# Input norm of a decoder trunk: squares on two engines, the first weights' load behind a copy, one exponential behind the last root

## The chip, the cores and the metric

The kernel runs on one core of one Trainium2 chip. A core has five engines with an instruction queue each: TensorE (PE, matrix products and transposes), VectorE (DVE), ScalarE (ACT), GpSimd (POOL) and SyncE (SP, which only issues DMAs here). Each engine takes its own instructions strictly in order, and semaphores make them wait for one another. The metric is the device time of one launch in microseconds. Three runs of the kernel before took 1421.04, 1417.68 and 1419.02 us.

## The reference

All data are float32, with SEQ = 512 rows of D_MODEL = 1024. A gated DeltaNet layer comes first, then an MLP with a short convolution, a K/V projection that is made once, an attention layer with a sliding window, a second MLP and a last norm. The change touches the very start, the norm of the input and what hangs on it:

```python
def rmsnorm(x, w):
    xf = x.astype(jnp.float32)
    y = xf * lax.rsqrt(jnp.mean(xf * xf, axis=-1, keepdims=True) + EPS)
    return (y * w.astype(jnp.float32)).astype(x.dtype)

def gated_deltanet(hn, w_in, conv_w, a_log, dt_bias, out_norm_w, w_out):
    proj = hn @ w_in
    qkv, z, b, a = jnp.split(proj, ...)
    qkv = jax.nn.silu(causal_dwconv(qkv, conv_w))
    q, k, v = jnp.split(qkv, [GDN_QK_DIM, 2 * GDN_QK_DIM], axis=-1)
    ...
    beta = jax.nn.sigmoid(b)
    g = -jnp.exp(a_log) * jax.nn.softplus(a + dt_bias)
    o = chunked_gated_delta_rule(q, k, v, g, beta)
    o = rmsnorm(o, out_norm_w) * jax.nn.silu(z)
    return o.reshape(bsz, t, GDN_V_DIM) @ w_out
```

## The kernel before

**Products.** Each float32 operand is split into a high part (rounded to the format that TensorE takes at full rate) and a low part (the rest). A product is three matmuls, high by high, low by high and high by low: L162, L163 and L164 in `mm3`, whose names `xh`, `xl` are the split input and `whi`, `wlo` the split weights. A projection of 128 columns sums over KD = 8 blocks of rows, so it is 24 matmuls into one PSUM bank `d` (128x512). Weights come in pieces of 256 columns into `stage` (two buffers, 1 MB each), and `cast` makes `whi` on ScalarE (L132) and `wlo` on VectorE (L133), 128 columns at a time, in three buffers each.

**The opening.** SP loads x in four pieces `xt` of 128 rows (L204, 512 KB each), then the first weights in two halves (L210). For each piece a square with a row sum (L258) and a root (L259) run on ScalarE, a reciprocal (L260) and the scaling (L261) on VectorE. TensorE transposes the scaled pieces (L266) into eight banks of four blocks each. `split_scaled` writes `xh` on ScalarE (L172) and `xl` on VectorE (L173). `columns` (L226 to 238) loads small vectors, transposes them (L235) and copies them out (L237): `normc` is the norm's weight, `cwc` the convolution's, and `onwc` and `fcw` others.

**After it.** The first projections are `d` of keys (128 columns each), then the gates (48 columns, weights `gst`, loaded by ScalarE's own queue in two transfers with runs of 64 bytes, L309 and L310). `conv_silu` takes a first tap on ScalarE (L277), three taps on VectorE (L280) and Silu on ScalarE (L281). The gate chain runs Sigmoid (L325), Abs (L326), Relu (L330), Exp (L327) and Ln (L328) on ScalarE, then an addition (L331), a product with `nega` (L332; `nega` is the exponential of a_log, L319), running sums (L335) and differences (L338) on VectorE, and copies to `gr` (L344 to L347). Functions of different tables on ScalarE need a table load between them, shown as ACT_TABLE_LOAD.

**The delta rule** works on four groups of heads: a triangular inverse built by levels (L576 to L615: products of 32x32 and 64x64 blocks on TensorE, with copies `pz` and `p6s` on ScalarE and writes into `sy` on VectorE between them), and a scan over four blocks of rows (L635 to L679). Projections for the next group stand between its steps on TensorE. Behind the last group the output projection multiplies `kT` and `qT` (high and low part of the gated output, which comes back from memory) by the next weights.

**What sets the order.** The kernel is written against a tile framework whose scheduler orders the instructions of each engine from a table of steps (ORDER, SHIFT), from its own estimate of when each could start, and from `behind(later, earlier)`, which fixes an order of issue and adds no wait. An edit at the start can therefore move instructions much later.

## Time and profile before

| what | value |
|---|---|
| runs of the kernel before | 1417.68, 1419.02, 1421.04 us (median 1419.02) |
| the profiled execution: its time, its span | 1418.66 us, 1416.8 us |
| granted TensorE clock, mean | 0.998 |
| TensorE busy | 1384.8 us, 98% |
| VectorE busy | 1109.1 us, 78% |
| ScalarE busy | 748.0 us, 53% |
| GpSimd busy | 15.7 us, 1% |

The span runs from the first to the last instruction; the profiled execution's time is 1.9 us longer than its span. "Busy" is the time in which an engine executes something. A group's row names the line, the engine, the operation and the tiles (output, arrow, inputs). In the timeline each row has start, duration and, in brackets, how long the engine was idle before and what ended the idle time.

### The profile page before, as it was taken

To read this page: it belongs to the slowest core of one execution; us is meant where nothing else is said; L and a number is where in the kernel's file an instruction comes from. 1 tells how busy PE (TensorE), PEld (TensorE's weight loads), DVE (VectorE), ACT (ScalarE), POOL (GpSimd) and SP (SyncE) were. 2 spreads that over 40 slices of the span, in tenths; PEclk is the share of its full clock that TensorE was granted. 3 is DMA by queue.
4 is the path that set the end of the run, shared out by engine and by line. 5 is a ranking of instruction groups with operands and counts; after the bars stand their busy time and mean duration, and the time that the engine had idled before them with its cause. 6 is when DMAs were issued, how large, how long until landed. Compare 5 with 4: busy or idle time off the path is not lost.

```text
span 1416.8 us, 21740 instructions
## 1 busy us (share of the span) xinstructions
PE 1384.8 (98%) x8362; PEld 1166.5 (82%) x8362; DVE 1109.1 (78%) x2072; ACT 748.0 (53%) x1470; POOL 15.7 (1%) x37
## 2 busy tenths in 40 slices
PE   7999999999999999999999999999999999999997
PEld 5787888878877888888988889778788888988897
DVE  4996886968856447879878889788658888878996
ACT  7764576656647325444335446567544444444543
POOL 1000000000100000000000000000000000000000
PEclk9999999999999999999999999999999999999999
DMA  5333254172465323221443223322132221432222
GB/s 160 90 104 115 80 174 124 60 230 84 143 221 157 119 86 115 90 90 46 134 149 119 75 73 108 109 76 76 60 112 86 93 90 59 137 107 86 95 75 75
DMA packets 162299, 151.80 MB, mean 107 GB/s; under 512 B 24148, under 2 KB 150677, under 8 KB 162197
## 3 DMA queue, kind: packets, MB, share of 16 engines
q1 hardware_dynamic: 159938, 150.22, 33.0%
q8 instruction: 66, 1.08, 0.3%
q10 hardware_dynamic: 2259, 0.20, 0.1%
q14 instruction: 36, 0.29, 0.1%
HBM read 133.60 MB, written 15.75 MB: 105 GB/s over the span
## 4 chain that ended last, share of the span: by engine, by line
PE 85%; DVE 7%; DMA 4%; ACT 2%; issue 1%; SPq 0%; DVEq 0%; ACTq 0%
PE d L162 20%; PE d L164 20%; PE d L163 20%; PE g L198 2%; DVE wlo L133 2%; PE d L1207 1%; PE d L1211 1%; PE d L1209 1%; PE d L1054 1%; PE d L1052 1%; PE d L1053 1%; PE s L1054 1%; PE p L1303 1%; PE s L659 1%; PE s L1052 1%
## 5 line engine op out<-in xcount | busy, mean ns | idle before, releaser
L162 PE MATMUL d<-xh,whi 128*128 128x512 f32 x1128 | 444.2, 394 | 0.2
L163 PE MATMUL d<-xl,whi 128*128 128x512 f32 x1128 | 444.0, 394 | 0.0
L164 PE MATMUL d<-xh,wlo 128*128 128x512 f32 x1128 | 442.1, 393 | 0.8 <-DVE wlo L133 0.5
L132 ACT CAST whi<-stage 128x1024 fp32r<-128x1024 f32 (+2 forms) x234 | 227.4, 976 | 249.7 <-PE d L163 170.3
L133 DVE TENSOR_TENSOR wlo<-stage,whi 128x1024 fp32r<-128x1024 f32 (+2 forms) x234 | 263.3, 1128 | 70.2 <-ACT whi L132 69.3
L164 PEld LDWEIGHTS d<-xh,wlo 128*128 128x128 f32 x1128 | 211.6, 188 | 45.5 <-DVE wlo L133 1.0
L162 PEld LDWEIGHTS d<-xh,whi 128*128 128x128 f32 x1128 | 211.7, 188 | 44.8 <-ACT xh L172 0.5
L163 PEld LDWEIGHTS d<-xl,whi 128*128 128x128 f32 x1128 | 211.7, 188 | 43.1 <-issue 0.5
L280 DVE SCALAR_TENSOR_TENSOR acc<-d,cwc,acc 128x511 f32<-128x511 f32 (+2 forms) x96 | 70.6, 738 | 8.7 <-ACT acc L277 7.8
L913 DVE TENSOR_TENSOR sz<-d,p6s 128x512 f32<-128x512 f32 x59 | 40.6, 688 | 43.4 <-PE d L164 41.2
L935 ACT ACTIVATE dt<-dt 128x512 f32<-128x512 f32 x44 | 27.8, 632 | 78.3 <-DVE dt L918 78.3
L918 DVE SCALAR_TENSOR_TENSOR dt<-sz,fcw,dt 128x511 f32<-128x511 f32 (+1 forms) x60 | 44.8, 747 | 1.8 <-ACT dt L916 0.9
L918 DVE SCALAR_TENSOR_TENSOR va<-sz,fcw,va 128x511 f32<-128x511 f32 (+1 forms) x58 | 43.3, 747 | 0.9
L561 DVE TENSOR_TENSOR sT<-sT,p6s 64x31 f32<-64x31 f32 (+15 forms) x124 | 40.9, 330 | 2.0
L555 DVE TENSOR_TENSOR p6s<-sN,sT 64x31 f32<-64x31 f32 (+15 forms) x124 | 40.7, 328 | 1.9
L1276 ACT ACTIVATE dt<-dt,sm 128x256 f32<-128x256 f32 (+1 forms) x64 | 30.1, 471 | 21.5 <-DVE sm L1259 21.5
L132 ACT CAST whi<-st 128x768 fp32r<-128x768 f32 (+1 forms) x30 | 23.7, 791 | 30.1 <-PE p L1053 5.8
L913 DVE TENSOR_TENSOR zl<-d,p6s 128x512 f32<-128x512 f32 x29 | 20.0, 688 | 17.8 <-PE d L164 17.8
L682 ACT ACTIVATE rq<-o 128x128 f32<-128x128 f32 x64 | 19.0, 301 | 25.0 <-DVE o L677 22.0
L937 DVE TENSOR_TENSOR va<-dt,va 128x512 f32<-128x512 f32 x44 | 30.4, 690 | 1.2
L133 DVE TENSOR_TENSOR wlo<-st,whi 128x768 fp32r<-128x768 f32 (+1 forms) x30 | 26.8, 899 | 2.2 <-ACT whi L132 2.2
L916 ACT ACTIVATE dt<-sz,normc,fcw 128x512 f32<-128x512 f32 x30 | 24.4, 815 | 6.5 <-DVE sz L913 6.2
(769 smaller groups left out, 2873.2 us busy)
## 6 DMA issues: line engine op xcount, KB each, us to landing
stage<-in_ffn_w_up_dram SPq DMA_DIRECT2D x44, 1024.0 KB, 4.7
stage<-in_a_w_in_dram SPq DMA_DIRECT2D x23, 1024.0 KB, 5.5
stage<-in_ffn_w_down_dram SPq DMA_DIRECT2D x16, 768.0 KB, 4.3
stage<-in_a_w_out_dram SPq DMA_DIRECT2D x8, 1024.0 KB, 5.1
st<-in_ffn_w_down_dram SPq DMA_DIRECT2D x8, 768.0 KB, 5.2
zd<-sz SPq DMA_DIRECT2D x16, 256.0 KB, 2.6
od<-o SPq DMA_DIRECT2D x16, 256.0 KB
stage<-in_b_w_q_dram SPq DMA_DIRECT2D x4, 1024.0 KB, 5.0
```

The lines of the kernel that those rows point to most:

```text
L132: S.copy(hi[:, :kt, :m], src)
L133: V.tensor_tensor(lo[:, :kt, :m], src, hi[:, :kt, :m].bitcast(F32), op=ALU.subtract)
L162: PE.matmul(ps, hi[:, k, :m], xh[k], start=first and k == 0, stop=False)
L163: PE.matmul(ps, hi[:, k, :m], xl[k][:], start=False, stop=False)
L164: done.append(PE.matmul(ps, lo[:, k, :m], xh[k], start=False, stop=last and k == kt - 1))
L280: V.scalar_tensor_tensor(acc[:, d:], ps[:, : T - d], col, acc[:, d:], op0=ALU.mult, op1=ALU.add)
L555: V.tensor_tensor(tv, N[:, s, s + 1 : 32].unsqueeze(2).to_broadcast([64, n, m]), Tm[:, s : s + 1, 0:m].to_broadcast([64, n, m]), op=ALU.mult,)
L561: V.tensor_tensor(Tm[:, s + 1 : 32, 0:m], Tm[:, s + 1 : 32, 0:m], tv, op=ALU.subtract)
L913: V.tensor_tensor(u[:], ps[:], rs[:], op=ALU.mult)
L918: V.scalar_tensor_tensor(acc[:, d:], u[:, : T - d], tap(2 - d, t), acc[:, d:], op0=ALU.mult, op1=ALU.add)
L937: V.tensor_tensor(b[:], a[:], b[:], op=ALU.mult)
L1276: S.activation(ej, ej, AF.Exp, bias=ngm[:, i : i + 1], scale=-1.0, accum_out=den[:, i : i + 1])
```

## The change

It does three things. The first weights' load is issued behind a copy on ScalarE, which reads two columns of the third x piece and writes two elements of the stage buffer, so that the load must wait for that copy (and the copy for the piece). The squares of the second and fourth piece (c = 1 and 3) run on VectorE as a product with a running sum, with the sum read out by a second instruction; the others stay on ScalarE. The exponential for `nega` is put behind the last root in the order of issue.

```diff
--- before.py
+++ after.py
@@ -205,14 +205,16 @@
         xs.append(xt)
     win = a_w_in[0]
     first = wpool.tile([P, 8, 256], F32, tag="stage", bufs=2, name=nm("stage"))
+    held_stage = {HQK * P: first}
+
+
+    ident = const([P, P], s="ident")
+    make_identity(nc, ident[:])
+
+    S.copy(first[:, 0, 0 : P + 1 : P], xs[2][:, 0:2])
     for i in range(2):
         cs = slice(HQK * P + i * P, HQK * P + (i + 1) * P)
         SP.dma_start(first[:, :, i * P : (i + 1) * P], win[:, cs].rearrange("(k p) c -> p k c", p=P))
-    held_stage = {HQK * P: first}
-
-
-    ident = const([P, P], s="ident")
-    make_identity(nc, ident[:])
     identr = const([P, P], F32R, s="identr")
     S.copy(identr[:], ident[:])
     ones = const([P, P], s="ones")
@@ -255,8 +257,21 @@
     for c in range(NC):
         junk = main.tile([P, D], F32, tag="nt", bufs=2, name=nm("junk"))
         r = const([P, 1], s="rx")
-        S.activation(junk[:], xs[c], AF.Square, accum_out=r[:])
-        S.activation(r[:], r[:], AF.Sqrt, bias=epsc[:, 0:1], scale=1.0 / D)
+
+        if c % 2 == 0:
+            S.activation(junk[:], xs[c], AF.Square, accum_out=r[:])
+        else:
+            V.tensor_tensor_reduce(
+                out=junk[:],
+                in0=xs[c][:],
+                in1=xs[c][:],
+                scale=1.0,
+                scalar=0.0,
+                op0=ALU.mult,
+                op1=ALU.add,
+                accum_out=r[:],
+            )
+        root = S.activation(r[:], r[:], AF.Sqrt, bias=epsc[:, 0:1], scale=1.0 / D)
         V.reciprocal(r[:], r[:])
         V.tensor_scalar(xs[c][:], xs[c][:], r[:, 0:1], None, op0=ALU.mult)
     xh, xl = [], []
@@ -316,7 +331,7 @@
     SP.dma_start(gp16[32:48, 0:1], a_a_log.rearrange("a h -> h a"))
     SP.dma_start(gp16[32:48, 1:2], a_dt_bias.rearrange("a h -> h a"))
     nega = const([48, 1], s="nega")
-    S.activation(nega[32:48, :], gp16[32:48, 0:1], AF.Exp)
+    behind(S.activation(nega[32:48, :], gp16[32:48, 0:1], AF.Exp), root)
     V.tensor_scalar(nega[32:48, :], nega[32:48, :], -1.0, None, op0=ALU.mult)
     R = row("sz")
     G.memset(R[0:80, :], 0.0)
```

Lines move by 2 near the start and by 15 behind the norm: the square is L262 (ScalarE) or L264 (VectorE, printed as ISA, with `rx` its sum), the root L274, the reciprocal L275, the scaling L276, the transposes L281, the taps L292 and L295, the addition L346, the differences L353, the levels L600 to L630, the scan's products L666 and L674. All names get a number one higher.

**The opening on VectorE**, from behind the two constants up to the first `xl`. xt_70, xt_72, xt_74 and xt_76 are the four pieces. Before:

```order
L260 RECIPROCAL rx_105<-rx_105 128x1
L261 TENSOR_SCALAR xt_70<-xt_70,rx_105 128x1024
L260 RECIPROCAL rx_111<-rx_111 128x1
L261 TENSOR_SCALAR xt_72<-xt_72,rx_111 128x1024
L260 RECIPROCAL rx_117<-rx_117 128x1
L261 TENSOR_SCALAR xt_74<-xt_74,rx_117 128x1024
L237 COPY normc_102<-g_100 128x128
L260 RECIPROCAL rx_123<-rx_123 128x1
L261 TENSOR_SCALAR xt_76<-xt_76,rx_123 128x1024
L133 TENSOR_TENSOR wlo_209<-stage_78,whi_208 128x1024
L173 SCALAR_TENSOR_TENSOR xl_134<-s_128,normc_102,xh_133 128x512
```

With the change, up to the first weights' low part:

```order
L264 ISA junk_111,rx_112<-xt_72 128x1024
L264 ISA rx_112 128x1
L275 RECIPROCAL rx_106<-rx_106 128x1
L276 TENSOR_SCALAR xt_70<-xt_70,rx_106 128x1024
L275 RECIPROCAL rx_112<-rx_112 128x1
L276 TENSOR_SCALAR xt_72<-xt_72,rx_112 128x1024
L275 RECIPROCAL rx_118<-rx_118 128x1
L264 ISA junk_123,rx_124<-xt_76 128x1024
L264 ISA rx_124 128x1
L239 COPY normc_103<-g_101 128x128
L276 TENSOR_SCALAR xt_74<-xt_74,rx_118 128x1024
L275 RECIPROCAL rx_124<-rx_124 128x1
```

The square of the second piece stands ahead of everything; that of the fourth stands between the reciprocal and the scaling of the third.

**The opening on ScalarE**, from the third piece to the first `xh`. whi_208 or whi_209 is the first projection's weight, whi_247 or whi_248 the gates'. Before:

```order
L258 ACTIVATE junk_116,rx_117<-xt_74 128x1024
L259 ACTIVATE rx_117<-rx_117,eps_90 128x1
L217 CAST identr_86<-ident_81 128x128
L258 ACTIVATE junk_122,rx_123<-xt_76 128x1024
L309 DMA gst_243<-in_a_w_in_dram 128x8x16
L259 ACTIVATE rx_123<-rx_123,eps_90 128x1
L132 CAST whi_208<-stage_78 128x1024
L310 DMA gst_243<-in_a_w_in_dram 128x8x16
L172 ACTIVATE xh_133<-s_128,normc_102 128x512
```

With the change:

```order
L214 COPY stage_78<-xt_74 128x2
L262 ACTIVATE junk_117,rx_118<-xt_74 128x1024
L274 ACTIVATE rx_118<-rx_118,eps_91 128x1
L219 CAST identr_87<-ident_79 128x128
L324 DMA gst_244<-in_a_w_in_dram 128x8x16
L325 DMA gst_244<-in_a_w_in_dram 128x8x16
L274 ACTIVATE rx_124<-rx_124,eps_91 128x1
L132 CAST whi_209<-stage_78 128x1024
L132 CAST whi_248<-gst_244 128x8x48
L172 ACTIVATE xh_134<-s_129,normc_103 128x512
```

The cast of the gates' weights has moved from behind the fifth `xh` to a place ahead of the first, and the second gate transfer from behind a weight cast to right behind the first transfer.

**The gate chain on VectorE**, from the third projection's weights to the fourth's; acc_236 and acc_413 are conv rows, va and sz the gate chain, wlo_545 and wlo_636 the low weights of the third and fourth projection of keys and queries. Before:

```order
L280 SCALAR_TENSOR_TENSOR acc_236<-d_207,cwc_204,acc_236 128x511
L280 SCALAR_TENSOR_TENSOR acc_236<-d_207,cwc_204,acc_236 128x510
L280 SCALAR_TENSOR_TENSOR acc_236<-d_207,cwc_204,acc_236 128x509
L133 TENSOR_TENSOR wlo_545<-stage_541,whi_544 128x1024
L133 TENSOR_TENSOR wlo_636<-stage_632,whi_635 128x1024
L331 TENSOR_TENSOR va_284<-va_284,va_289 16x512
L280 SCALAR_TENSOR_TENSOR acc_413<-d_384,cwc_204,acc_413 128x511
L332 TENSOR_SCALAR va_289<-va_284,nega_279 16x512
L280 SCALAR_TENSOR_TENSOR acc_413<-d_384,cwc_204,acc_413 128x510
L335 SCALAR_TENSOR_TENSOR sz_282<-ones_88,va_289 16x128 x4
L338 TENSOR_SCALAR sz_282<-sz_282 16x128 x4
```

With the change, from the second tap of the first conv row:

```order
L295 SCALAR_TENSOR_TENSOR acc_237<-d_208,cwc_205,acc_237 128x510
L133 TENSOR_TENSOR wlo_546<-stage_542,whi_545 128x1024
L295 SCALAR_TENSOR_TENSOR acc_237<-d_208,cwc_205,acc_237 128x509
L295 SCALAR_TENSOR_TENSOR acc_414<-d_385,cwc_205,acc_414 128x511
L346 TENSOR_TENSOR va_285<-va_285,va_290 16x512
L295 SCALAR_TENSOR_TENSOR acc_414<-d_385,cwc_205,acc_414 128x510
L347 TENSOR_SCALAR va_290<-va_285,nega_280 16x512
L295 SCALAR_TENSOR_TENSOR acc_414<-d_385,cwc_205,acc_414 128x509
L350 SCALAR_TENSOR_TENSOR sz_283<-ones_89,va_290 16x128 x4
L353 TENSOR_SCALAR sz_283<-sz_283 16x128 x4
L133 TENSOR_TENSOR wlo_637<-stage_633,whi_636 128x1024
L133 TENSOR_TENSOR wlo_672<-stage_633,whi_671 128x1024
```

wlo_636 stood ahead of the chain; as wlo_637 it stands behind all of it.

**The same place on TensorE**, at the start of the fourth projection, with d_634 or d_635 its bank. Before:

```order
L162 MATMUL d_634<-xh_133,whi_635 128x512
L163 MATMUL d_634<-xl_134,whi_635 128x512
L164 MATMUL d_634<-xh_133,wlo_636 128x512
L162 MATMUL d_634<-xh_142,whi_635 128x512
L163 MATMUL d_634<-xl_143,whi_635 128x512
L164 MATMUL d_634<-xh_142,wlo_636 128x512
```

With the change:

```order
L162 MATMUL d_635<-xh_134,whi_636 128x512
L163 MATMUL d_635<-xl_135,whi_636 128x512
L162 MATMUL d_670<-xh_134,whi_671 128x512
L163 MATMUL d_670<-xl_135,whi_671 128x512
L164 MATMUL d_635<-xh_134,wlo_637 128x512
L162 MATMUL d_635<-xh_143,whi_636 128x512
L163 MATMUL d_635<-xl_144,whi_636 128x512
```

Two products of the projection behind it have been put ahead of the first that needs wlo_637.

**The last group of the delta rule on TensorE**, near 407 to 411 us of the profile before, with p_4050 and s_4061 the last level's banks, s_4133 the scan's first product. Before:

```order
L605 MATMUL p_4050<-Xg,nt_3418 64x64 x8
L162 MATMUL d_4404<-xh_169,whi_4405 128x512
L163 MATMUL d_4404<-xl_170,whi_4405 128x512
L164 MATMUL d_4404<-xh_169,wlo_4406 128x512
L612 MATMUL s_4061<-sy_4001,p6s_347 64x64 x8
L651 MATMUL s_4133<-vt_3773,sy_3929 128x128 x2
L162 MATMUL d_4404<-xh_178,whi_4405 128x512
L651 MATMUL s_4133<-vt_3866,sy_4001 128x128 x2
L163 MATMUL d_4404<-xl_179,whi_4405 128x512
L164 MATMUL d_4404<-xh_178,wlo_4406 128x512
L162 MATMUL d_4404<-xh_187,whi_4405 128x512
L163 MATMUL d_4404<-xl_188,whi_4405 128x512
```

With the change, from the same product on:

```order
L620 MATMUL p_4051<-Xg,nt_3419 64x64 x8
L627 MATMUL s_4062<-sy_4002,p6s_348 64x64
L666 MATMUL s_4134<-vt_3774,sy_3930 128x128 x2
L627 MATMUL s_4062<-sy_4002,p6s_348 64x64 x7
L162 MATMUL d_4626<-kT_4479,whi_4627 128x512
L162 MATMUL d_4684<-kT_4479,whi_4685 128x512
L163 MATMUL d_4626<-qT_4480,whi_4627 128x512
L164 MATMUL d_4626<-kT_4479,wlo_4628 128x512
L163 MATMUL d_4684<-qT_4480,whi_4685 128x512
L162 MATMUL d_4626<-kT_4479,whi_4627 128x512
L666 MATMUL s_4134<-vt_3867,sy_4002 128x128 x2
```

The products of the last gate projection that stood between the levels now run earlier, and six of the output projection (d_4626, d_4684) stand there.

## Prediction

> **What bounds the kernel now.** I read four views in this order: the page's busy shares and chain of waits, the table of what TensorE waited for, the busy time in windows of 40 us, and the timeline of the opening, of 30 to 46 us and of 410 to 426 us.
>
> ```profile
> span 1416.8 us, 21740 instructions
> PE 1384.8 (98%) x8362; PEld 1166.5 (82%) x8362; DVE 1109.1 (78%) x2072; ACT 748.0 (53%) x1470; POOL 15.7 (1%) x37
> ...
> PE 85%; DVE 7%; DMA 4%; ACT 2%; issue 1%; SPq 0%; DVEq 0%; ACTq 0%
> ```
> ```profile
> engine line waited for: us in total, times, longest us
> PE g L235 <- DMA xt<-in_x_dram: 8.5, 1, 8.5
> ...
> PE d L162 <- ACT kT L168: 2.0, 1, 2.0
> PE g L235 <- DVE onwc L237: 1.7, 1, 1.7
> PE g L198 <- ACT ol L720: 1.5, 1, 1.5
> PE p L659 <- ACT us L653: 1.5, 1, 1.5
> ```
> ```profile
> 0.00:40.00 40.00, 30.56 (x134) 23.04 (x135) 21.01 (x36) 29.72 (x45) 6.01 (x17) 1.00 0.45 142
> 40.00:80.00 40.00, 38.25 (x197) 31.02 (x196) 37.07 (x75) 30.95 (x68) 0.00 (x0) 1.00 0.39 114
> ...
> 280.00:320.00 40.00, 38.48 (x266) 30.43 (x266) 29.03 (x56) 22.96 (x47) 0.00 (x0) 1.00 0.66 204
> ...
> 400.00:440.00 40.00, 36.56 (x326) 30.19 (x325) 23.43 (x52) 24.11 (x75) 0.61 (x2) 1.00 0.65 212
> ```
>
> TensorE (PE) is busy 1384.8 of 1416.8 us, and its work is the same afterwards, so the new time is the old one plus the change in its idle time. The idle is 9.4 us before 40 us, 1.75 at 40 to 80, 1.5 at 280 to 320 and 3.4 at 400 to 440 (window less its first busy figure). The waits name each: 8.5 until the input, 1.7 for the copy of onwc, 1.5 for the scaled ol, 2.0 and 1.5 inside the last group of the delta rule. The change reorders instructions up to about 440 us; behind that the order is unchanged, so an idle microsecond won or lost before then reaches the end whole.
>
> **The opening, as it runs.** The timeline's columns are start, duration, engine, line, operation, and in brackets the wait:
>
> ```profile
> 8.16 1.06 ACT L258 ACTIVATE junk<-xt 128x1024 f32<-128x1024 f32 x1 [0.94 <-DMA xt<-in_x_dram]
> ...
> 9.34 0.29 ACT L259 ACTIVATE rx<-rx,eps 128x1 f32<-128x1 f32 x1
> ...
> 9.73 1.05 ACT L258 ACTIVATE junk<-xt 128x1024 f32<-128x1024 f32 x1
> ...
> 9.87 0.75 DVE L261 TENSOR_SCALAR xt<-xt,rx 128x1024 f32<-128x1024 f32 x1
> ...
> 10.92 0.40 ACTq L310 DMA_DIRECT2D gst<-in_a_w_in_dram  x1
> ...
> 11.11 1.03 ACT L132 CAST whi<-stage 128x1024 fp32r<-128x1024 f32 x1
> ...
> 11.44 0.75 DVE L261 TENSOR_SCALAR xt<-xt,rx 128x1024 f32<-128x1024 f32 x1
> ...
> 12.17 1.23 DVE L133 TENSOR_TENSOR wlo<-stage,whi 128x1024 fp32r<-128x1024 f32 x1
> ...
> 12.89 0.69 ACT L172 ACTIVATE xh<-s,normc 128x512 fp32r<-128x512 f32 x1 [0.75 <-PE s L266]
> ...
> 13.62 0.75 DVE L173 SCALAR_TENSOR_TENSOR xl<-s,normc,xh 128x512 fp32r<-128x512 f32 x1 [0.22 <-ACT xh L172]
> 13.63 0.80 PE L162 MATMUL d<-xh,whi 128*128 128x512 f32 x1
> ...
> 16.16 0.50 ACT L132 CAST whi<-gst 128x384 fp32r<-128x384 f32 x1
> ...
> 18.29 0.39 PE L162 MATMUL d<-xh,whi 128*128 128x512 f32 x1
> ```
> ```profile
> 0.00:8.00 8.00, 0.00 (x0) 0.00 (x0) 1.07 (x5) 4.15 (x8) 4.14 (x13) 1.00 0.75 273
> ```
>
> **Weights held back: worth nothing to x.** In the first 8 us the core moved 273 GB/s x 8 us = 2.18 MB. The four pieces of x are 2.10 MB and the constants of ScalarE's queue 0.07, so the weights, issued behind x on the same queue, had not begun. The last square starts at 9.73 without waiting for x4: ScalarE was only then free. So x lands as before. [...] The copy (128x2, estimated 0.2 us from the page's small ScalarE rows such as the 0.29 root) starts when the third piece is there, 8.16; SP then issues the weights at about 8.4 rather than 4.27, and they land an estimated 0.3 to 1 us later, about 11.5. The weight cast started at 11.11 and now stands behind a root at 11.7, which covers it.
>
> **Squares on VectorE: a loss of about 1.1 us to the first product.** No row shows the reduce at this size. Its bounds are 0.75 (a VectorE pass of 128x1024 with one input, L261) and 1.92 (four times the 480 ns that a custom VectorE reduction takes for 128x256); I take 1.23, from the two-input pass of the same size (L133), plus 0.1 for reading the accumulator:
>
> ```profile
> L1259 DVE CUSTOM_DVE_ANT_0 dt<-s,sz,nsink x40: 344/479/484, 934.5 to 1004.6; 128x256 f32<-128x256 f32 x30, 128x128 f32<-128x128 f32 x10
> ```
>
> The square of x2 is hidden (5.7 to 7.0, while x3 still moves). That of x4 is not, since VectorE's order puts it behind the reciprocal of piece 3 and ahead of piece 3's scaling. The square of x3 on ScalarE ends 0.2 later for the copy, so its root ends at 9.8 and the reciprocal at 10.0; the square of x4 runs 10.05 to 11.4; normc's copy follows; scaling of x3 starts at 11.7 (before: 9.87); root, reciprocal and scaling of x4 end at 13.3 (before: 12.19). Four transposes later xh starts at about 14.0 against 12.89. On ScalarE the cast of the gate weights (0.50, formerly 16.16) now stands ahead of that xh, at about 13.5: their second transfer is issued some 0.5 earlier than 10.92, so I cost it at nothing, covered by the wait for x4.
>
> From the first product to 18.29 TensorE has little slack, but part of it ran slow: 0.80 for the product at 13.63 against 0.39 at 18.29. If the fast clock comes at the same absolute time, about 16, some 0.65 is won back. One gates product goes ahead into a wait (0.23, the spacing of products). So the dense stretch starts 1.1 - 0.65 = 0.45 later and the gates end 0.25 later. Bounds: +0.1 and +1.4 (nothing won back, 0.3 more for the gate cast). The exponential behind the last root costs nothing either way: before, it stood at 18.29, behind all roots already; it now stands two xh earlier, and all xh are still ready ahead of their products.
>
> **The gate chain: TensorE's new wait.** The next weights leave 1.5 earlier (their SP issue waited for the gates' wlo, which moves ahead of two xl), without use: the cast had other waits. The rows of the second place:
>
> ```profile
> 26.47 1.28 ACT L281 ACT_TABLE_LOAD   x1
> ...
> 31.60 1.28 ACT L327 ACT_TABLE_LOAD   x1
> ...
> 34.61 1.28 ACT L328 ACT_TABLE_LOAD   x1
> 34.63 1.23 DVE L133 TENSOR_TENSOR wlo<-stage,whi 128x1024 fp32r<-128x1024 f32 x1 [6.92 <-ACT whi L132]
> ...
> 36.66 0.68 DVE L331 TENSOR_TENSOR va<-va,va 16x512 f32<-16x512 f32 x1 [0.81 <-ACT va L328]
> ...
> 39.57 0.39 PE L164 MATMUL d<-xh,wlo 128*128 128x512 f32 x1
> ...
> 40.89 0.87 DVE L338 TENSOR_SCALAR sz<-sz 16x128 f32<-16x128 f32 x4
> ...
> 45.96 0.48 PE L235 MATMUL g<-ident,f 128*128 128x128 f32 x2 [1.72 <-DVE onwc L237]
> ```
>
> Before, wlo of the fourth projection ran at 34.63, five us ahead of its product at 39.57. Now it stands behind the whole gate chain on VectorE. That chain starts 0.45 later, loses about 1.2 because wlo of the third projection (1.23) slips between its first taps, so that the Silu table (26.47), which waits for the last tap, loads at 27.3 or later; between Exp and Ln a conv row (0.69) replaces a weight cast (1.05), -0.4. The addition then starts at 37.0 (36.66), a tap each stands between the steps as before, and the four L338 rows end near 42.0 (41.76). wlo runs 42.0 to 43.2. TensorE reaches the product at 39.57 + 0.25 + two pulled-ahead products (0.46) = 40.3 and waits **2.9 us**. In return the 1.72 at 45.96 goes: the rows between (13 products, 2.96, the transposes 0.6, two products 0.46) bring TensorE to fcw at 47.3, and onwc, behind two wlo, gr, a tap and a third wlo (1.2 + 0.7 + 0.7 + 1.2 = 3.9 behind 43.2), is there at 47.2. So 47.3 against 45.96: **+1.4 us**, which holds the opening's shift. Bounds +0.6 (chain at its old time) and +2.9 (the opening at its upper bound carries through).
>
> **280 to 440 us.**
>
> ```profile
> 299.98 1.21 PE L198 MATMUL g<-ident,ol 128*128 128x128 f32 x4 [1.52 <-ACT ol L720]
> ```
> ```profile
> 409.02 0.87 DVE L615 TENSOR_TENSOR sy<-sy,s 64x256 f32<-64x256 f32 x2 [1.78 <-PE s L612]
> ...
> 418.03 0.71 PE L659 MATMUL p<-us,ktok 128*128 128x128 f32 x4 [1.45 <-ACT us L653]
> ...
> 426.23 0.73 PE L162 MATMUL d<-kT,whi 128*128 128x512 f32 x2 [1.98 <-ACT kT L168]
> ```
>
> At 300 us two products now stand ahead of the transposes: -0.45. In the last group, 15 products (3.4 us) that filled the waits between the levels of the triangular inverse have been used up before, and six of the output projection (1.4) come in; 2.0 of wait open. On VectorE a wlo, a qT and zl (1.23 + 0.69 + 0.75) go ahead of L615, which had 1.78 of idle: 0.9 more. Against this, kT is cast earlier: -1.98. Net +0.9, with bounds of -3.4 (both late waits go, no new one opens) and +2.9 (only new ones). Sum: 1.4 - 0.45 + 0.9 = **+1.9**. On the profiled execution's own 1418.66 (span 1416.8 plus 1.9 around it) that is 1420.5; the median of the three runs is 1419.02, 0.36 above it, and I give 1420.7 between the two sums.
>
> **Rivals.**
> 1. *The opening slips by a clock window (slower).* The slow products at 13.63 turn fast about 16, some 3 us after TensorE became dense. If dense work now begins 1.1 later and the fast clock follows it, nothing is won back, and the gates' transfer late by 1 us would add to it. The opening then gives +1.1 to +2.1 rather than 0.45, the total 1421.3 to 1422.3; it passes 1421.9 when xh starts behind 14.6. For it: the gate cast now stands ahead of all xh. [...] Chance 0.15.
> 2. *The wait for wlo and the unfilled levels both at their upper bounds (slower)*: decided by the last group alone, if the levels cost +2.9 and kT's wait stays: 1418.7 + 1.4 - 0.45 + 2.9 = 1422.6. Chance 0.2.
> 3. *The new order closes the late waits (faster).* 1.52, 1.45 and 1.98 go, 4.95 in all, and the early +1.4 stands: 1415.1 to 1415.5; half of it gives 1417.6. For it: kT's cast stands ahead of the us copy now. Against it: us has no new filler. Chance 0.14.
> 4. *The hold does free the input*: x4's last descriptors come earlier by up to 1 us because the engines aren't shared. Then all of the opening is 0.5 to 1 earlier and the total about 1419.7. The 2.18 MB speak against it. Chance 0.06.
> 5. *Nothing reaches the end*: wlo comes in time, the levels neither win nor lose: 1419.0 within 0.5. Chance 0.1.
>
> The forecast has 0.35. A measurement of this kernel tells 0.2% (2.8 us) from no change, so "same" is 1416.2 to 1421.9. The forecast falls there with 0.26 of its 0.35, rival 1 with 0.08, rival 2 with 0.04, rival 3 with 0.04, rivals 4 and 5 whole: same 0.58, slower 0.32, faster 0.10. The range goes from a little beyond half of rival 3 (1417.2) to the upper bounds of the early part and of the last group together (1418.7 + 2.9 - 0.45 + 2.9 = 1424.1).
>
> **What would show it.** Right: the first DVE square near 5.7 lasting about 1.2, the second near 10; first xh near 14.0; a wait of TensorE for wlo of about 3 us at 40; no wait for onwc; no 2.0 for kT. Wrong: xh at or ahead of 12.9, wlo ahead of its product, or new idle between 80 and 280 us, where before there was next to none and I have set nothing.

## The result and the profile after

The changed kernel took 1427.88 us (median of four runs, 1425.67 to 1428.55) against 1418.35 for the kernel before beside it (1415.40 to 1421.04): a ratio of 1.0065, interval 1.0042 to 1.0088. It is slower by 9.5 us. The two profiled spans, 1425.7 and 1416.8, differ by 8.9.

The page of the changed kernel, span and busy times:

```profile
span 1425.7 us, 21745 instructions
PE 1391.6 (98%) x8362; PEld 1169.3 (82%) x8362; DVE 1110.3 (78%) x2076; ACT 747.8 (52%) x1468; POOL 13.3 (1%) x37
```

Set this against the page before. TensorE's idle time (span less busy) went from 32.0 to 34.1 us: +2.1. Its busy time went from 1384.8 to 1391.6 with the same 8362 products: +6.8. So three quarters of the loss isn't waiting: as many products, of the same shapes, kept TensorE busy for longer.

The waits of TensorE (engine, line, what it waited for, us in total, times, longest):

```profile
PE g L237 <- DMA acc<-in_ffn_conv_b_dram: 9.5, 1, 9.5
...
PE d L164 <- DVE wlo L133: 2.8, 1, 2.8
PE d L162 <- ACT xh L172: 2.2, 1, 2.2
...
PE s L627 <- ACT p6s L623: 1.0, 2, 0.5
PE p L674 <- ACT us L668: 0.9, 2, 0.7
PE s L607 <- ACT pz L603: 0.8, 1, 0.8
```

New are 2.8 for wlo, 2.2 for xh and the short waits between the levels (p6s, pz), and the first wait is 9.5 where it was 8.5. Gone are 1.7 for onwc and 2.0 for kT; ol (1.5 before) is at 0.5 and us (1.5 before) at 0.9.

The opening in the timeline (start, duration, engine, line, operation, wait in brackets):

```profile
5.60 1.23 DVE L264 CUSTOM_DVE_ANT_0 junk<-xt 128x1024 f32<-128x1024 f32 x1 [4.59 <-DMA xt<-in_x_dram]
6.75 0.08 DVE L264 DVE_READ_ACCUMULATOR2_ANT rx<- 128x1 f32 x1
...
7.97 0.19 ACT L214 COPY stage<-xt 128x2 f32<-128x2 f32 x1 [0.81 <-DMA xt<-in_x_dram]
...
9.66 1.21 DVE L264 CUSTOM_DVE_ANT_0 junk<-xt 128x1024 f32<-128x1024 f32 x1
9.79 0.73 ACTq L325 DMA_DIRECT2D gst<-in_a_w_in_dram  x1
...
11.84 0.75 DVE L276 TENSOR_SCALAR xt<-xt,rx 128x1024 f32<-128x1024 f32 x1
...
12.06 1.05 ACT L132 CAST whi<-stage 128x1024 fp32r<-128x1024 f32 x1 [0.86 <-DMA stage<-in_a_w_in_dram]
...
14.80 0.51 ACT L132 CAST whi<-gst 128x384 fp32r<-128x384 f32 x1 [1.69 <-DMA gst<-in_a_w_in_dram]
15.22 0.68 ACT L172 ACTIVATE xh<-s,normc 128x512 fp32r<-128x512 f32 x1
...
15.95 1.22 PE L162 MATMUL d<-xh,whi 128*128 128x512 f32 x2 [2.19 <-ACT xh L172]
...
19.39 0.78 PE L162 MATMUL d<-xh,whi 128*128 128x512 f32 x1
...
22.22 0.39 PE L162 MATMUL d<-xh,whi 128*128 128x512 f32 x1
```

x itself is ready: its last scaling runs at 11.84, and the first weights are cast at 12.06. Then ScalarE stands still for 1.69 us in front of the gates' weights, which aren't needed yet, and the first xh stands behind them in its queue: 15.22 against 12.89. The first product is at 15.95 against 13.63, and products still take 0.78 at 19.39. The first at 0.39 that is shown is at 22.22; before, it was at 18.29.

The granted clock shows a good part of the rest. In each profile the records of TensorE's clock change between 1.0 and 0.5 at multiples of 3.413 us from one another (before: 1396.05 us at 1.0, 409 times 3.413; changed: 395.95 at 1.0, 6.83 at 0.5 and 996.69 at 1.0, which are 116, 2 and 292 times), except for the last stretch at the kernel's end. The windows below are cut on that grid, counted from the start of the first stretch at full clock (21.9 us in the changed kernel, 16.4 before). Ahead of that stretch there is no record, and the view prints 1.00 there although the products are slow (0.78 us at 19.39). The columns are the window and its length, then busy time and count of PE, PEld, DVE, ACT and POOL, the granted clock, DMA share and GB/s. Changed:

```profile
42.34:45.76 3.42, 1.79 (x7) 0.86 (x5) 3.29 (x11) 2.56 (x4) 0.00 (x0) 1.00 0.01 2
45.76:49.17 3.41, 2.20 (x10) 1.82 (x11) 3.35 (x4) 2.48 (x4) 0.00 (x0) 1.00 0.01 4
...
414.40:417.81 3.41, 1.90 (x84) 1.52 (x82) 1.57 (x4) 2.63 (x4) 0.00 (x0) 1.00 0.51 147
417.81:421.22 3.41, 2.90 (x33) 2.37 (x30) 2.98 (x5) 1.44 (x4) 0.30 (x1) 0.50 0.50 146
421.22:424.64 3.42, 3.42 (x14) 2.72 (x11) 2.78 (x5) 0.62 (x1) 0.00 (x0) 0.50 0.50 159
424.64:428.05 3.41, 3.20 (x24) 2.53 (x22) 0.68 (x2) 1.72 (x3) 0.00 (x0) 1.00 1.02 346
```

Before, the same two places (the levels of the last group stand at 402 to 409 here):

```profile
43.66:47.07 3.41, 1.69 (x9) 1.03 (x7) 3.41 (x9) 3.38 (x5) 0.00 (x0) 1.00 0.17 31
...
402.06:405.47 3.41, 3.41 (x82) 2.57 (x83) 1.58 (x3) 1.35 (x4) 0.00 (x0) 1.00 0.75 230
405.47:408.88 3.41, 3.41 (x79) 2.45 (x68) 1.25 (x3) 1.33 (x3) 0.30 (x1) 1.00 0.54 190
...
415.71:419.12 3.41, 1.96 (x17) 1.77 (x17) 1.87 (x3) 3.31 (x10) 0.00 (x0) 1.00 0.86 266
422.54:425.95 3.41, 1.71 (x12) 1.29 (x10) 1.13 (x4) 1.82 (x7) 0.00 (x0) 1.00 0.87 289
```

Before, the levels' many small products (82 and 79 rows) had full-size ones between them, and both windows are busy throughout; now the window at 414.40, with 84 rows, is busy for 1.90 of 3.41. In the changed kernel's last group of the delta rule the clock is at half rate from 417.81 to 424.64, 6.8 us. What that does to the products can be read off their rows: 128x512 products that follow one another start 0.43 us apart there (422.55 to 423.83), against 0.23 at full rate (18.29 to 18.76 before). In the kernel before it stays at full rate from 16.4 us to the tail, although single windows there are idle for 1.72 and 1.70 us.

A table by place: the start of the n-th product of TensorE in each profile, less that in the profile before, as time won or lost in each stretch; in brackets how much of it is TensorE's idle time. The stretches end at product 200 (54.9 us before), product 4000 (668.9) and the last, counted from 0; the n-th product isn't the same one in every kernel, so the inner ends are good to about half a microsecond. For e2 its ten added products are counted out of the numbering, but their time (some 2.3 us) is in its second column.

| kernel | to product 200 | 200 to 4000 | to the end | at half clock after the opening, us |
|---|---|---|---|---|
| changed | +4.9 (idle +3.4) | +5.5 (+0.2) | -1.2 (-1.2) | 6.8 at 418 |
| e1, gate cast late | +4.2 (+1.7) | +4.9 (+0.1) | -1.4 (-1.3) | 3.4 at 46; 10.2 at 415 |
| e2, last group filled | +4.6 (+2.4) | +7.0 (+0.8) | -0.3 (-0.5) | 3.4 at 46; 3.4 at 435 |
| e3, copy alone | +3.1 (+1.0) | +5.2 (-0.1) | -0.7 (-0.5) | 3.4 at 45; 10.2 at 414 |
| e4, squares alone | +6.2 (+3.5) | +5.1 (+0.2) | -0.7 (-0.6) | 3.4 at 48; 6.8 at 420 |
| e5, wlo early | +1.9 (+0.9) | +2.5 (+1.1) | -0.5 (-0.1) | none |
| e6, all repaired | +1.6 (-0.4) | +1.4 (-0.7) | -1.3 (-1.0) | 3.4 at 304 |
| e7, holes in the kernel before | +0.8 (+0.1) | +1.4 (-0.6) | -0.9 (-0.7) | 3.4 at 46; 3.4 at 414 |
| e10, late pins | +5.6 (+4.0) | +12.8 (+3.1) | -0.6 (-0.2) | 3.4 at 47; 17.1 at 412 |

### The profile page after: what moved, and what is told of

It reads as the page before. It is cut to its first block, busy times and chain, and to the rows that moved or that the text cites. A ratio compares the mean times of both kernels' runs of the same rounds, so it can differ in the third digit from the quotient of the medians.

```text
span 1425.7 us, 21745 instructions
## 1 busy us (share of the span) xinstructions
PE 1391.6 (98%) x8362; PEld 1169.3 (82%) x8362; DVE 1110.3 (78%) x2076; ACT 747.8 (52%) x1468; POOL 13.3 (1%) x37
## 4 chain that ended last, share of the span: by engine, by line
PE 85%; DVE 6%; DMA 3%; ACT 2%; issue 1%; DVEq 0%; SPq 0%; ACTq 0%
PE d L164 19%; PE d L162 19%; PE d L163 19%; PE g L198 2%; DVE wlo L133 1%; PE d L1069 1%; PE d L1222 1%; PE d L1226 1%; PE d L1224 1%; PE d L1067 1%; PE d L1068 1%; PE s L1069 1%; PE s L1067 1%; PE s L1068 1%; PE s L666 1%
## 5 line engine op out<-in xcount | busy, mean ns | idle before, releaser
L295 DVE SCALAR_TENSOR_TENSOR acc<-d,cwc,acc 128x511 f32<-128x511 f32 (+2 forms) x96 | 70.6, 739 | 17.0 <-ACT acc L292 8.5
L928 DVE TENSOR_TENSOR sz<-d,p6s 128x512 f32<-128x512 f32 x59 | 40.6, 689 | 42.2 <-PE d L164 39.9
L933 DVE SCALAR_TENSOR_TENSOR va<-sz,fcw,va 128x511 f32<-128x511 f32 (+1 forms) x58 | 43.4, 747 | 0.9
```

The source lines that it names most:

```text
L295: V.scalar_tensor_tensor(acc[:, d:], ps[:, : T - d], col, acc[:, d:], op0=ALU.mult, op1=ALU.add)
L928: V.tensor_tensor(u[:], ps[:], rs[:], op=ALU.mult)
L933: V.scalar_tensor_tensor(acc[:, d:], u[:, : T - d], tap(2 - d, t), acc[:, d:], op0=ALU.mult, op1=ALU.add)
```

## The experiments

Two explanations stood against each other. One: the reduce on VectorE and the late weights cost the time themselves, in the opening. The other: they hardly matter, and the order that the scheduler makes of them costs it, at three places: the gate cast ahead of xh, wlo of the fourth projection behind the gate chain, and the last group without its filler. Each experiment is shown as its edit to the changed kernel or to the kernel before; `behind(later, earlier)` fixes an order of issue and adds no wait.

### e1, the gate cast late

```diff
-    gw = cast(gst, KD, 0, m=48)
+    gw = cast(gst, KD, 0, m=48, after=scaled_xh[4])   # behind(S.copy of whi, xh[4])
```

> The changed kernel, with the cast of the gate weights put behind the fifth xh in the order of issue (it then stands behind the last). Theory A, the first xh waits behind that cast for a late transfer, TensorE idles 2.2 us and its clock rises late: first xh at 13.1 to 13.6 instead of 15.22, TensorE's wait for xh (2.2) under 0.6, full clock by 16 to 19 us instead of 21.8, and 2 to 3.5 us less than the changed kernel's 1427.9: 1424.4 to 1425.9. Rival B, the squares on VectorE bring the fourth piece too late by themselves: first xh at 14.5 or later, under 1 us gained. Rival C, the wait moves to the gate chain (its weights come later): first xh early, but the end of the wait for wlo near 47 stays, 1427 to 1428.

Measured: 1427.41 us against 1417.48, ratio 1.0073 (1.0047 to 1.0098). No gain in the median, though the opening is repaired; 1424.4 to 1425.9 had been expected for that. Timeline of e1, the first xh and the wait for wlo; then its windows:

```profile
13.26 0.68 ACT L174 ACTIVATE xh<-s,normc 128x512 fp32r<-128x512 f32 x1
...
44.60 0.51 PE L166 MATMUL d<-xh,wlo 128*128 128x512 f32 x1 [2.75 <-DVE wlo L135]
```
```profile
42.73:46.14 3.41, 1.54 (x7) 1.28 (x8) 3.35 (x6) 3.13 (x5) 0.00 (x0) 1.00 0.01 2
46.14:49.56 3.42, 3.42 (x12) 2.61 (x10) 2.13 (x3) 0.00 (x0) 0.00 (x0) 0.50 0.77 228
...
414.78:418.20 3.42, 2.19 (x64) 1.87 (x64) 1.89 (x5) 2.60 (x4) 0.00 (x0) 0.50 0.79 227
```

xh is 1.96 us earlier than in the changed kernel, and at product 120 (36.85 us before) the loss is 1.6 against 3.7. Then it comes back. The wait for wlo is 2.75 us in both. In the changed kernel the grid cut it in two, 1.63 us of idle in one window and 1.21 in the next, and the clock stayed. In e1 1.87 us fall into one window and the next window runs at half clock. In the last group e1 has 10.2 us at half clock, from 414.8 on, against 6.8. So the same wait had a second price in e1, 3.4 us at half clock, and none in the changed kernel; that it depends on where the grid stands is read off these two profiles.

### e2, the last group filled with throwaway products

```diff
+        warm_up(p3, 4, g, pr)    # in the last pair: 4, 3 and 3 products identr x xh[0]
+        warm_up(p6, 3, g, pr)    # ahead of the levels' own into the same bank
+        warm_up(p7, 3, g, pr)
```

> The changed kernel, with ten throwaway products of identity by the first xh (128x512) written into banks of the last group's levels ahead of their real use; their results are overwritten. Theory A, the holes between the levels let the granted clock fall to 0.5 for 6.8 us near 418, and that costs most of the late loss: clock 1.0 from 410 to 430, and 2 to 3.5 us less than the changed kernel: 1424.4 to 1425.9. Rival B, the late loss is the waiting itself, or the clock falls for another reason: no gain, up to 2.3 us slower (10 x 0.23), 1427.9 to 1430.

Measured: 1429.22, ratio 1.0084 (1.0061 to 1.0107). Not faster than the changed kernel. Windows of e2 over the levels, and later:

```profile
414.40:417.80 3.40, 3.40 (x55) 2.35 (x53) 0.91 (x3) 1.98 (x5) 0.00 (x0) 1.00 0.68 229
417.80:421.20 3.40, 3.35 (x77) 2.49 (x78) 3.26 (x6) 2.10 (x4) 0.30 (x1) 1.00 0.46 147
```
```profile
431.50:434.90 3.40, 1.42 (x12) 1.23 (x11) 2.02 (x6) 0.96 (x4) 0.00 (x0) 1.00 0.55 212
434.90:438.30 3.40, 3.40 (x9) 2.68 (x9) 0.47 (x2) 0.84 (x6) 0.00 (x0) 0.50 0.52 143
```

The filler did hold the clock through the levels. But it cost its own ten products (some 2.3 us at their spacing of 0.23), and a wait of 1.98 for the next gated output opened at 434.6 in place of the holes and took the clock down there for 3.4 us. As a price of the holes this run is inconclusive: throwaway work that fills a hole costs its own time.

### e3 and e4, the copy alone and the squares alone

```diff
 e3 (to the kernel before)
+    S.copy(first[:, 0, 0 : P + 1 : P], xs[2][:, 0:2])   # and the first weights' load behind it
 e4 (to the kernel before)
+        else: V.tensor_tensor_reduce(...)               # for c = 1 and 3
```

> Only the copy that holds the first weights back; squares on ScalarE as before. Its order keeps the gate cast behind the fourth xh, but has wlo of the fourth projection behind the gate chain and the holes in the last group, as the changed kernel has. Theory A, the reordering costs, place by place: opening +0.3 to +1 against before, wait for wlo of 2.5 to 3.2 us at 40 less the 1.7 for onwc, the clock falls to 0.5 in the last group: 1422 to 1425 against 1418.4. Rival B, late weights are what costs: 1427 to 1428, as the changed kernel. Rival C, only the squares cost: 1418 to 1419.

> Only the squares of the second and fourth piece on VectorE, the first weights loaded as before. Its order has the gate cast and one more weight cast (1.05) ahead of the first xh, wlo behind the gate chain and the holes in the last group. Theory A: first xh at 14.5 to 16.5 (12.89 before), TensorE's wait ahead of it 1.5 to 3.5, a wait for wlo, the clock falls late: 1427 to 1430. Rival B, late weights are what costs: 1419 to 1421. If the clock holds in the last group in spite of the holes: 1424 to 1426.

Measured: e3 1426.39, ratio 1.0062 (1.0043 to 1.0081); e4 1430.20, ratio 1.0091 (1.0069 to 1.0112). Each alone costs as much as both. Each gives the same later order, with wlo behind the gate chain and the last group without its filler. The exponential's pin, alone or beside the others, moves no instruction on any engine in the built programs, so it has no run. Timeline of e3:

```profile
12.89 0.80 PE L162 MATMUL d<-xh,whi 128*128 128x512 f32 x1 [0.38 <-ACT xh L172]
...
43.52 0.50 PE L164 MATMUL d<-xh,wlo 128*128 128x512 f32 x1 [2.75 <-DVE wlo L133]
```

e3 is the telling one. It has no square on VectorE, and its gate cast stands behind the fourth xh, out of the way of the first: the first product is 0.7 us earlier than before (the third piece of x was there at 6.94, 8.14 before). It is 0.5 us behind at product 120. And yet its last product starts 7.6 us later, with the same wait of 2.75 and 13.6 us at half clock. Its 1426.39 is slower than the 1422 to 1425 that the second explanation gave it and lies in none of the three ranges; e4's 1430.20 is just above its 1427 to 1430. The first explanation falls: neither the squares nor a late opening are needed for the loss.

### e5 and e6, the order put back in the changed kernel

```diff
 e5 (to the changed kernel)
+    behind(made["ln"], made["cast"][4][0])    # the fourth projection's whi ahead of Ln
+    behind(made["add"], made["cast"][4][1])   # its wlo ahead of the gate chain's addition
 e6 (e5, and)
+    behind(made["cast"][1][0], made["xh"][4])   # gate cast behind the fifth xh
+    behind(made["z15"][1][1], made["p1"])       # last gate projection between
+    behind(made["z15"][0][3], made["p3"])       # the levels of the last pair
+    behind(made["z15"][0][4], made["p6"])
```

> The changed kernel, with both casts of the fourth projection's weights put ahead of Ln and of the addition in the order of issue, where they stood before. The order then follows the kernel before from about 60 us on, the last group's products between its levels too; the opening stays the changed one, gate cast ahead of the first xh. Theory A, everything behind the opening was lost through this one place: no wait for wlo over 0.6 us near 40, granted clock 1.0 from 22 us to the end, and 1.7 to 3.7 us above the kernel before, 6 to 8 below the changed one: 1419 to 1421.5. Rival B, the late loss has its own cause in the changed opening: clock falls in the last group all the same, 1423 to 1426.

> As the run before, and the gate cast behind the fifth xh as well (what the change itself asks for is all there: squares on two engines, weights held back, exponential behind the last root). Theory A, only the order cost: first xh near 13.3, 0.4 to 1.7 us above the kernel before: 1417.9 to 1419.5. Rival B, the late weights or VectorE's squares cost by themselves: 1421 or more.

Measured against 1418.75: e5 1421.35, ratio 1.0018 (1.0009 to 1.0028); e6 1420.87, ratio 1.0011 (0.9997 to 1.0024). The two pins of e5 bring 1.0065 down to 1.0018, about 6.7 of the 9.5 us. They also bring back, without being told to, TensorE's order before from product 295 on (75 us), with the filler in the last group. The waits of e5:

```profile
PE d L166 <- ACT xh L176: 2.2, 1, 2.2
PE d L166 <- ACT kT L172: 2.1, 1, 2.1
PE g L202 <- ACT ol L741: 2.0, 1, 2.0
PE p L678 <- ACT us L672: 1.5, 1, 1.5
```

The old late waits are back (kT 2.1, ol 2.0, us 1.5), the wait for wlo is gone, the opening's 2.2 for xh is still there, and there is no half-clock stretch after 19.6 us. More idle time than in the changed kernel between products 200 and 4000 (+1.1 against +0.2), and 3 us less time: the 6.8 us at half clock, worth at most 3.4, are what is gone. e6 takes the gate cast away too. It lies between its two expected ranges and its interval holds 1: with the old order, two squares on VectorE and late weights cost between nothing and 3.4 us.

### e7, the holes alone, in the kernel before

```diff
+    behind(made["p1"], made["z15"][1][7])   # the last gate projection wholly ahead of the last pair's levels
```

> The kernel before, with one pin: the products of the last gate projection stand ahead of the last pair's levels (as in the changed kernel), so that the levels have no products between them. Nothing ahead of 380 us changes. Theory A, the holes let the clock fall: granted clock 0.5 for 6.8 to 10.2 us near 410, 3 to 5 us slower than before: 1420.5 to 1422.5. Rival B, the holes cost only their waiting: TensorE's idle time grows by as much as the time, clock 1.0. Rival C, free: 1417 to 1418.5.

Measured: 1421.38 against 1418.75, ratio 1.0021 (1.0010 to 1.0032), so 3.0 us (1.4 to 4.5). Its windows:

```profile
42.17:45.58 3.41, 1.68 (x10) 1.07 (x8) 3.38 (x6) 3.36 (x6) 0.00 (x0) 1.00 0.00 0
45.58:48.99 3.41, 3.41 (x14) 3.03 (x14) 2.31 (x7) 1.80 (x4) 0.00 (x0) 0.50 0.94 289
...
410.81:414.22 3.41, 2.37 (x44) 1.89 (x37) 3.13 (x5) 2.25 (x4) 0.30 (x1) 1.00 0.59 223
414.22:417.63 3.41, 3.16 (x11) 2.42 (x12) 1.44 (x3) 0.59 (x1) 0.00 (x0) 0.50 0.60 184
```

From product 200 to 4000 it has less idle time than the kernel before (0.6 less) and takes 1.4 us more. All eleven runs tell the same: their mean granted clock is 0.9948 on average against 0.9973 in the 29 runs of the kernel before, about 3.5 us of clock against 3.0 of time, and among the eleven the slower runs are by and large those with the lower clock (1418.63 at 0.997, 1424.93 at 0.992). And the old wait for onwc, 1.72 us, which did no harm in the kernel before, left 1.73 us of one window idle here, and the clock fell.

### e10, the changed kernel with the last gate projection pinned late

```diff
+    behind(made["z15"][1][1], made["p1"])   # as in e6, without the pins on wlo and the gate cast
+    behind(made["z15"][0][3], made["p3"])
+    behind(made["z15"][0][4], made["p6"])
```

> The changed kernel with one repair alone: the products of the last gate projection pinned between the levels of the last group, where they stood before. Opening and wait for wlo stay. Theory A, the holes and the clock that falls in them cost 3 to 5 us of the changed kernel's 9: granted clock 1.0 from 380 to 440, 1423 to 1425. Rival B, the waits of kT and us come back in their place (2.0 and 1.5): 1426 to 1428, clock 1.0.

Measured: 1437.34 against 1418.66, ratio 1.0127 (1.0107 to 1.0147): the slowest of all, far beyond both expected ranges. It was meant to fill the holes in the new order. The pins held the filler back from the pair before, so that pair's levels stood open instead:

```profile
408.63:412.05 3.42, 1.68 (x52) 1.00 (x51) 2.58 (x3) 0.66 (x3) 0.00 (x0) 1.00 0.87 302
412.05:415.46 3.41, 2.45 (x40) 2.08 (x42) 1.25 (x3) 0.73 (x2) 0.30 (x1) 0.50 0.90 291
...
422.29:425.70 3.41, 3.41 (x25) 2.42 (x21) 0.00 (x0) 0.73 (x2) 0.30 (x1) 0.50 0.57 170
```

The clock fell at 412.0 and stayed at half for 17.1 us, five windows on end, though the later four are wholly busy, most of them in part with the levels' small products. Of the 12.8 us lost between products 200 and 4000, 3.1 are idle time.

### e8, e9, e11 and e12, an early clock for the kernel before

In the kernel before, the products between 13.63 and 16.4 are slow (0.80 us for the row at 13.63, 0.39 at 18.29). Could it be made faster by giving TensorE something to do from the start? Each of the four adds throwaway products of the identity by itself (128x128, two rows each in the trace: x144 for 72 in e8) behind the identity's making, and pins the order after it.

```diff
+    for _ in range(72):   # e8; 36 in e9; 16, and 17 behind the norm weights' transpose, in e11; 16 and 12 in e12
+        PE.matmul(turn_on[:, 0:P], ident[:], ident[:], start=True, stop=True)
 e11: normc's copy ahead of the last reciprocal, the first wlo behind the last scaling
 e12: e11, and nsink behind the last xl
```

> The kernel before, with 72 throwaway products of identity by identity (128x128) on TensorE while it waits for x, and the order behind held near that of before by the pins of the run before. Theory A, the clock rises with sustained work wherever it comes from: full clock by 6 to 9 us, transposes and first products at full rate, dense stretch 1.5 to 2.5 us earlier: 1415 to 1416.5. Rival B, TensorE still waits for the fourth piece at 12 us and the clock falls there again: 1417 to 1418.5.

> As the early clock run, with 36 throwaway products instead of 72. Those 72 ended at 20.3 us and held the transposes back until then; at 0.22 us each, 36 fewer end near 12.3, when the fourth piece is scaled. Theory A, an early clock is worth the slow transposes and products: full clock by 7 us and kept, first xh at 12.4 to 13.0, dense products 0.8 us earlier than in the kernel before, 0.5 to 2.5 us faster than it: 1416.3 to 1418.3 against 1418.8. Rival B, gained time is given back at the wait for onwc near 46 or later: within 0.5 us of the kernel before.

> The kernel before with 16 throwaway products ahead of the transposes of the norm's weight and 17 behind, and that weight's copy and the first wlo pinned where they stood on VectorE (in the run with 36, TensorE waited 3.2 us for the copy and its clock fell at 17.4). The order behind is near that of the kernel before. Theory A: no wait over 1 us behind the first transpose, full clock by 7.5 us and kept to the end, first xh at 12.3 to 13.0, dense products 0.5 to 1.5 us earlier: 1416.5 to 1418.5. Rival B, the clock can be had early, but the wait for the fourth piece drops it again or other waits take the gain: 1418.5 to 1420.

> As the split early clock, with nsink (which waited until 17.2 for its own load and stood ahead of the first xl) pinned behind the last xl, and 12 throwaway products instead of 17 behind the norm's transposes. Theory A, one instruction that waits for a late load ahead of the first xl undid the early clock: no wait of TensorE over 1 us between 12 and 30, dense products 0.3 to 1 us ahead of the kernel before, and 1416.5 to 1418.5 if the clock keeps to the end. Rival B, the dense start moves but the order behind 45 us loses it again (a fall of the clock near 304, as in the last run, +1.7 to 2): 1418.5 to 1420.

Measured: e8 1424.03, ratio 1.0035 (1.0022 to 1.0048); e9 1425.90, 1.0048 (1.0031 to 1.0065); e11 1423.36, 1.0036 (1.0024 to 1.0049); e12 1417.77 against 1418.36, 0.9994 (0.9984 to 1.0003). Timeline rows of e8, e9, e11 and e12, one or two each:

```profile
1.79 18.65 PE L222 MATMUL p<-ident 128*128 128x128 f32 x144 [1.79 <-POOL ident masks.py:199]
```
```profile
17.32 1.03 PE L273 MATMUL g<-ident,xt 128*128 128x128 f32 x4 [3.24 <-DVE normc L244]
```
```profile
17.21 0.17 DVE L750 TENSOR_SCALAR nsink<-sink 128x16 f32<-128x16 f32 x1 [3.49 <-DMA sink<-in_b_sinks_dram]
17.29 0.75 DVE L177 SCALAR_TENSOR_TENSOR xl<-s,normc,xh 128x512 fp32r<-128x512 f32 x1
```
```profile
1.78 5.72 PE L223 MATMUL p<-ident 128*128 128x128 f32 x32 [1.78 <-POOL ident masks.py:199]
...
13.75 0.48 PE L166 MATMUL d<-xh,whi 128*128 128x512 f32 x1
```

The clock came at 5.8 to 7.4 us in all four (16.4 before). e8 has too many: the throwaways run to 20.4 and hold the transposes back. In e9 and e11 one small instruction for a constant of a much later stage (nsink) stood ahead of normc's copy or of the first xl on VectorE, and waited 3.49 us for its transfer. All three came out slower than both of their expectations. It is the same fault as the changed kernel's gate cast, on another engine. e12 takes it out of the way; the first product runs in 0.48 instead of 0.80, and at product 200 the profile is 1.9 us ahead. In the stretch after that it loses 3.0, with a window at half clock at 299.3. At the end its profile is 0.4 us ahead. So e12 is the same as the kernel before within the measurement, and no version here beats it.

## Why the prediction was wrong, step by step

**The sum's first sentence failed.** It said that TensorE's work stays the same and that the new time is the old one plus the change in idle time. The 6.8 us of longer products had no term in it. The forecast +1.9 of idle time against +2.1 in the pages is luck as a total: up to product 200 idle time rose by 3.4 where the sum has 1.4, and 1.2 behind product 4000, which it doesn't have, came off again. And the signs that I had named (the squares, the wait for wlo, none for onwc, none for kT) came out as said, all but xh: they watched waits, and none watched the clock. At half rate products stand 0.43 apart instead of 0.23, so 6.8 us at half clock in the last group cost at most 3.4, and the late full clock of the opening some 1.6 (4.9 less 3.4 of idle). The rest, about 2 us, isn't settled; 1.3 of it lies between products 200 and 2400 (55 to 370 us before), all at full clock. A product's row lasts 0.39 while products follow one another at 0.23, so each break in a stream adds busy time without work; that would do it, but it is argued, not shown.

**Weights held back: right in this profile.** The copy started at 7.97, which puts the third piece at 7.97 against 8.16 before, 0.2 earlier and no more. But in the seven profiles with the hold that piece was there at 6.9 to 8.3, in the seven without it at 8.1 to 8.5: in two of them (e2 at 7.4, e3 at 6.9) it did come earlier, so "nothing" was too firm. The load left at 8.19 (I had 8.4) and landed at 12.06 (11.5), later than the root that was to cover it (10.90). ScalarE waited 0.86 for it, so there was no cover.

**Squares on VectorE: the price right, the consequence too long.** The reduce took 1.23 and its reading out 0.08; I had 1.23 and 0.1. The last scaling started at 11.84, which ends at 12.6 where I had 13.3. Without the gate cast, xh came at 13.26 (e1) where I had 14.0.

**The gate cast: the step that failed in the opening.** I costed it at nothing, "covered by the wait for x4", because its transfer is issued earlier. I didn't ask when it lands: 14.80, five us behind its issue at 9.79. In the kernel before the cast at 16.16 hadn't waited, so its row said nothing of the landing, and the bound of 0.3 that I gave it had no row behind it. It moved xh by 1.96 in one profile (15.22 against e1's 13.26) and by 1.77 in another pair (15.20 in e5, 13.43 in e6). In the runs neither pair shows a gain beyond the intervals. Rival 1 had the right effect, at 15.22 behind its point of 14.6, but its price (+1.1 to +2.1) was below the 3.7 at product 120.

**The gate chain: right.** The wait for wlo was forecast at 2.9 and is 2.75; the wait for onwc is gone, as forecast. Beyond the opening's shift the stretch from product 120 to 200 costs 1.25. I had 0.95 there (1.4 less the opening's 0.45). What I missed is the wait's second price, a half-clock window behind it, in e1 to e4 and e10; in the changed kernel's profile the grid spared it.

**The wait for ol at 300 us: closed, but nothing won.** From product 200 to 2400 idle time fell by 0.7 (I had 0.45), and the stretch still took 0.7 longer.

**The last group: waits right, the term mis-sized for want of the clock.** I counted its waits (+0.9, with -1.98 for kT in it), and from product 2400 to 3100 (370 to 473 us before) idle time rose by just that, 0.9. But the stretch costs 4.8. The 15 products that had filled the levels did more than cover waits: they kept the clock. With them gone, the window at 414.40 was idle for 1.51 us and filled otherwise with 84 products of 32x32 and 64x64, and the next two ran at half rate. e7 gives the price of the holes by themselves, 3.0 us (1.4 to 4.5) in the runs; in its profile the same stretch takes 1.9 longer with no more idle time and one window at half clock. e5, which has the filler back and the old waits too, has no half clock and loses 0.9 there. (TensorE's order differs up to 463 us, not 440 as I wrote; nothing hangs on it.)

**The exponential: right.** Its pin moves nothing.

Rivals 3, 4 and 5 didn't occur: of the late waits only kT and most of ol closed, x came only 0.2 earlier in this profile, and the early terms did reach the end. Rival 2 had the last group deciding, by waits; the place was right and the mechanism wrong: the granted clock was 0.50 there from 417.81 to 424.64. I used the clock for the slow products of the opening alone and didn't carry it to 400 us.

What stays open: how the 2.6 us that remain in e5 divide among the squares, the late weights and the gate cast, since e6's interval reaches from nothing to 3.4. e6's runs also scatter more than any others here (1415.5 to 1425.1), which their granted clock (0.997 to 0.999) doesn't account for. The 1.2 us that the changed kernel wins back behind product 4000 (all of it idle time) are hardly a gain of the change: every other profile here is 0.3 to 1.5 us shorter there than the one profile of the kernel before.

## What to carry to other kernels

Before costing a moved instruction at nothing, look at what stands behind it in its engine's queue and when the transfer that it reads has landed, not when it was issued; a row that didn't wait doesn't say how early its data were there. On this TensorE, 98% busy, a hole could cost more than its length: in e1 1.87 us of idle time in one window were followed by 3.4 us at half clock (in the changed kernel products stand 0.43 apart at that rate, 0.23 at full). A term for idle time alone was too small here. And products that filled holes and had to run anyway were worth more than the wait that they covered: e7, which has them earlier, took 3.0 us more (1.4 to 4.5), and its profile had 0.6 us less idle time from product 200 to 4000. Among the signs that would show a forecast right or wrong, name the busy time of the same work and the granted clock, not waits alone. When a small edit at the start of a scheduled kernel costs more than its own place can explain, put the old order back with a pin or two before blaming the edit: two pins gave back 6.7 of 9.5 us here.

## What the runs showed of the hardware

**The clock behind idle windows.** On each profile's own grid of 3.413 us, over the fourteen profiles, the windows behind the first full clock with more than 1.72 us of TensorE idle time are these (those at the kernel's end, where TensorE runs out of work, left out):

| idle, us | kernel and start of window | next window |
|---|---|---|
| 3.24, 2.03 | e9 at 14.0, 304.2 | half |
| 2.67 | e10 at 43.4 | half |
| 2.65, 1.98 | e2 at 42.4, 431.5 | half |
| 2.22 | e4 at 44.4 | half |
| 2.01 | e3 at 41.5 | half |
| 1.92, 1.86 | e11 at 427.3, 301.0 | half |
| 1.90 | e11 at 14.2 | full |
| 1.87 | e1 at 42.7 | half |
| 1.76 | e6 at 300.2 | half |
| 1.73 | e7 at 42.2 | half |

Twelve of thirteen were followed by a window at half rate. Just below, the kernel before had 1.72 and 1.70, e12 1.67 and 1.63, the changed kernel 1.63, e2 and e5 1.53, and the clock stayed. (The ends of TensorE's rows are modelled, so 1.72 and 1.73 are the same.) Below that it fell only in the last group's levels (after 1.71, 1.51, 1.37, 1.04, 0.86 and even 0.63 us of idle time, where the busy part is small products), once among transposes (e12, 1.33 at 295.9) and at the ends of e10 (1.70) and e6 (1.57). So in most of these rows the clock turned at about half a window of idle time (1.72 of 3.413 us), and among small products at less. What it goes by is not shown, since no run varied idle time or the size of the products by itself. One and the same wait, 2.7 to 2.8 us for wlo, was followed by a window at half clock in five kernels (e1 to e4 and e10, with 1.87 to 2.67 us of idle time in the window before) and by none in the changed kernel (1.63 and 1.21).

**The way back to full clock.** Of the windows at half rate, those that were followed by full clock had TensorE busy for 3.09 us or more of 3.41, and at most 0.6 us of that with products of 32x32 or 64x64. Half rate went on behind 2.90 us (changed kernel, 417.81), behind 2.96 us of transposes in the openings of e4 and e6 (read from the products behind them, which still take 0.78 us at 19.52 and 16.16, since no record stands there), and behind windows that were busy for 3.14 to 3.41 us with 1.05 to 1.9 us of small products (e3, e10). A fall among the levels lasted 6.8 to 17.1 us in five of six profiles, and a fall elsewhere inside the kernel 3.4. That is read off these windows, and no run varied it by itself.

**The kernel before stands close to these rows.** Its waits of 1.72 and 1.98 us leave 1.72 and 1.70 in their windows. In e7, whose grid stands elsewhere (42.17 against 43.66), the same wait of 1.72 left 1.73 in its window, and the next one ran at half rate.

**An early full clock.** With 32 rows of float32 identity products from 1.78 us on, e12 had the full clock at 5.8; the kernel before, without them, at 16.4.
